# Six weight blocks of the merge's output product: high and low part made by two DMAs and a negation

## The chip, the core and the metric

One Trainium2 chip, one of its cores. The metric is device time in microseconds (us) of one execution of the whole program; lower is better. Differences between two kernels are told by the median of several runs.

## The reference, cut to what matters

The reference is one layer of a decoder trunk for 512 prompt tokens and 8 sample tokens (520 columns in the kernel, in two halves of 260). After RMSNorm, a wide projection `w_in` feeds two branches: retention with four heads (branch A) and a gated MLP with spatial mixing (branch B). Then comes the merge and the channel part:

```
m = sigmoid(a_ret) * branch_ret + sigmoid(a_gm) * branch_gm
h = x + m @ w_o                                   # 1024 x 1024, the product that the change touches
hn = rms_norm(h)
h = h + (silu(hn @ w_gate) * (hn @ w_up)) @ w_ffn_down
y = rms_norm(h)
```

All inputs are float32, and the kernel keeps nearly float32 accuracy.

## The kernel before, in words

**How a product is computed.** TensorE works on float32r numbers (float32 rounded to fewer bits). Each float32 operand is split into a high part (rounded to float32r) and a low part (the rounded difference), and `product` (L102) sums three matmuls: high by high, high by low, low by high. One block of 128 output rows with a contraction over 1024 takes 48 matmuls of 128x128 by 260 columns.

**How weights arrive.** `weights` (L92) takes three tiles of 128x1024 float32: SP loads 512 KB into `wraw` (L98), ScalarE casts it into `whi` (L87), VectorE writes raw minus high into `wlo` (L90). Tiles come from pools by turns (`wtile`, L77): in the stages around the change there are five buffers of `wraw` (three in pool `wp`, two in pool `wq`), four of `whi` and four of `wlo`. So the high and low buffers of block i come free when TensorE has ended block i-4.

**The stages around the change.** First the product with `w_gm_o`, eight blocks (loop at L709): VectorE multiplies each result by a gate (L715), GpSimd adds branch A (L717; VectorE does the last one), and the sum is split into `m`. Four marking matmuls follow (L840). Then comes the output product with `w_o`, eight blocks (loop at L841 to L851): `xr` is loaded (L843), the weights come from `weights` (L844), 48 matmuls into `ps_wo`, of which two PSUM tiles exist; VectorE adds x and writes `hs` (L849), ScalarE squares it and GpSimd adds the squares up (`add_square`, L162, L165, L167).

**What follows.** The feed-forward input product takes seven combined products per block (`sum_weights` L736, `sum_acts` L765, `seven` L815, `ffn_in` L868). `sum_weights` puts its raw data into buffers of the same kind `wraw`: `s13` into the three of `wp` (two SP loads of 256 KB, L749, and a GpSimd DMA of 512 KB that adds to them, L750) and `ab` into the two of `wq` (SP, L752). VectorE then makes further sums from both (L758, L759), and every sum is split into `whi` and `wlo`. `sum_acts` prepares the activations from `hs` (ScalarE fills at L855, VectorE sums at L793 to L807, splits). These start while the `w_o` product still runs.

**The order on each engine.** Each engine runs its instructions in one fixed order. It is laid down when the program is built: the framework plays the program through a timeline of its own (`schedule_with_timeline_sim=True`) and lets each engine take, of the instructions that are ready in that plan, the earliest in the program. On the chip, an instruction whose data is late holds up all that stand behind it on its engine; a DMA issued by GpSimd stands in GpSimd's order, one by SP in SP's.

Of the kernel before, what the change touches and what calls it, by code (L numbers as in the profile page):

```python
# [7 lines left out]
F32 = mybir.dt.float32  # L8
F32R = mybir.dt.float32r
I32 = mybir.dt.int32  # L10
AF = mybir.ActivationFunctionType
ALU = mybir.AluOpType
# [3 lines left out]
KT = D // P  # L16
# [19 lines left out]
def halves(ap):  # L36
    return ap.rearrange("p (a b) -> p a b", a=2)
# [3 lines left out]
def step_kernel(ctx: ExitStack, tc: tile.TileContext, io):  # L41
    nc = tc.nc
# [13 lines left out]
    def ttile(name):  # L56
        return tmp.tile([P, T], F32, name=name, tag="tmp")
# [10 lines left out]
    def acc_psum(name):  # L68
        return psm.tile([P, 2, 512], F32, name=name, tag="mm")
# [4 lines left out]
    def ev(ps):  # L74
        return ps[:, :, 0:HT]

    def wtile(kind, dt=F32R):  # L77

        pools = wpools[kind]
        pool = pools[wturn[kind] % len(pools)]  # L80
        wturn[kind] += 1
        return pool.tile([P, 8 * P], dt, name=kind, tag=kind, bufs=pools.count(pool))

    def split(hi, lo, src, hi_eng=None, lo_eng=None):

        if hi_eng is None:
            nc.scalar.copy(out=hi, in_=src)  # L87
        else:
            hi_eng.tensor_copy(out=hi, in_=src)
        (lo_eng or nc.vector).tensor_tensor(out=lo, in0=src, in1=hi.bitcast(F32), op=ALU.subtract)  # L90

    def weights(src, n, cuts=()):  # L92

        raw, hi, lo = wtile("wraw", F32), wtile("whi"), wtile("wlo")
        at = [0, *cuts, n]
        for a, b in zip(at, at[1:]):
            sl = slice(a * P, b * P)
            nc.sync.dma_start(out=raw[:, sl], in_=src[:, sl])  # L98
            split(hi[:, sl], lo[:, sl], raw[:, sl])
        return hi, lo  # L100

    def product(ps, w, at, x, first, last, fs=(0, 1)):  # L102

        sl = slice(at * P, (at + 1) * P)
        wh, wl = w[0][:, sl], w[1][:, sl]
        for n, (a, k) in enumerate(((wh, 0), (wh, 1), (wl, 0))):
            for f in fs:
                nc.tensor.matmul(  # L108
                    (ps[f] if isinstance(ps, list) else ps[:, f])[:, 0:HT], a, x[:, k, f * HT : (f + 1) * HT],
                    start=first and n == 0, stop=last and n == 2,  # L110
                )
# [50 lines left out]
    def add_square(acc, src, first, add=None):  # L162

        q = acc if first else stile("sqr")
        nc.scalar.activation(out=q, in_=src, func=AF.Square)  # L165
        if not first:
            (add or nc.gpsimd).tensor_tensor(out=acc, in0=acc, in1=q, op=ALU.add)  # L167
# [53 lines left out]
    def z_tile(m, name, w=None):  # L221
        w = w or weights(io["w_in"][m], KT)
        ps = acc_psum(name)
        for kt in range(KT):
            product(ps, w, kt, xg[kt], kt == 0, kt == KT - 1)
        return ps
# [7 lines left out]
    rsqrt_table(ones_f)  # L234
    x_load(0)
    w_first = [weights(io["w_in"][0], KT, (2, 4))]
    x_split(0)
    x_load(1)
    x_load(2)
    x_split(1)  # L240
    x_split(2)
    w_first.append(weights(io["w_in"][1], KT, (4,)))
    for kt in range(3, KT):
        x_load(kt)
# [464 lines left out]
    for i in range(KT):  # L709
        w = weights(io["w_gm_o"][i], KT)  # L710
# [130 lines left out]
    for i in range(KT):  # L841
        xt = ttile("xr")
        nc.sync.dma_start(out=xt, in_=io["xT"][i * P : (i + 1) * P, :])  # L843
        w = weights(io["w_o"][i], KT)  # L844
        ps = acc_psum("ps_wo")
        for kt in range(KT):
            product(ps, w, kt, mm[kt], kt == 0, kt == KT - 1)
        hi = hs[:, i, :]
        nc.vector.tensor_tensor(out=halves(hi), in0=ev(ps), in1=halves(xt), op=ALU.add)  # L849
        if i < KT - 1:  # L850
            add_square(sq, hi, i == 0)  # L851
# [53 lines left out]
    def down_weights(i, k0, n):  # L905
        return weights(io["w_ffn_down"][i][:, k0 * P : (k0 + n) * P], n)
# [28 lines left out]
    i = KT - 1  # L935
    hi = hs[:, i, :]
    ps = [aux(f"ps_fd{f}") for f in range(2)]
    w = down_weights(i, k0, n)
# [116 lines left out]
```

## Time and profile before

| | |
|---|---|
| median of 3 runs | 1140.57 us (1140.07 to 1145.29) |
| the profiled execution, its own time | 1138.51 us |
| its span from first to last instruction | 1136.8 us |
| mean granted TensorE clock | 0.996 of full speed |
| TensorE busy | 1113.2 us, 98% of the span |
| VectorE, ScalarE, GpSimd busy | 67%, 45%, 20% of the span |
| DMA, mean over the span | 145 GB/s |

The profile's times are in microseconds from the start of the span; durations of single instructions are in nanoseconds where so marked. PE is TensorE's matmul, PEld its weight load, DVE VectorE, ACT ScalarE, POOL GpSimd, SPq and POOLq the queues on which SP and GpSimd issue DMAs. A bracket behind a row of the timeline says how long the engine sat idle before the instruction, and what ended that. `L90` is line 90 of the kernel. Tiles go by the program's names, `s` being the tile `s13` or `s24` of `sum_weights`.

### The profile page before, as it was taken

The numbers are of one execution on the slowest core, as the hardware profiler recorded it, in microseconds if no ns is written. First come the engines' busy times: TensorE is split into PE (matmuls) and PEld (weight loads), VectorE is DVE, ScalarE is ACT, GpSimd is POOL, SyncE is SP. The second block draws the span as 40 slices with busy tenths as digits, with TensorE's granted clock in tenths as the row PEclk, the third lists the DMA queues.
The fourth block names the chain that finished last, engine by engine and source line by source line (L and its number), as shares of the span: only waits on it lengthen the run. The fifth ranks groups of instructions, "written<-read, shape, count | busy, mean of one in ns | idle before, by whom it ended". The sixth has DMA issues, their size and how long they took to land.

```text
span 1136.8 us, 21703 instructions
## 1 busy us (share of the span) xinstructions
PE 1113.2 (98%) x8982; PEld 1092.4 (96%) x8982; DVE 763.0 (67%) x1225; ACT 512.6 (45%) x836; POOL 224.7 (20%) x197
## 2 busy tenths in 40 slices
PE   8999999999999999999999999999999999999995
PEld 7999999999999999999999999999999999999995
DVE  7778837884878478737544446598776468755655
ACT  6356346533643356423332442366564145532552
POOL 4303201320132011001311222132332013210110
PEclk9999999999999999999999999999999999999998
DMA  7267335733673367222222323565654557446212
GB/s 272 96 217 291 107 117 210 266 110 112 230 245 110 112 219 282 87 94 97 82 75 93 102 78 109 159 140 139 173 161 150 145 118 187 136 132 147 80 42 76
DMA packets 54450, 164.82 MB, mean 145 GB/s; under 512 B 6432, under 2 KB 8880, under 8 KB 54344
## 3 DMA queue, kind: packets, MB, share of 16 engines
q1 hardware_dynamic: 43504, 124.53, 32.8%
q0 software_dynamic: 10848, 38.91, 12.6%
q8 instruction: 70, 1.15, 0.4%
q14 instruction: 28, 0.23, 0.1%
HBM read 142.32 MB, written 21.10 MB: 144 GB/s over the span
## 4 chain that ended last, share of the span: by engine, by line
PE 82%; DVE 8%; DMA 4%; issue 2%; ACT 2%; POOL 1%; SPq 0%; DVEq 0%; ACTq 0%; POOLq 0%
PE ps_f L827 14%; PE ps_fd L108 10%; PE ps_ro L108 8%; PE ps_v L108 8%; PE ps_g L108 7%; PE ps_gv L108 4%; PE ps_gu L108 4%; PE ps_ar L108 4%; PE ps_gm L108 4%; PE ps_ag L108 4%; PE k L108 3%; PE q L108 3%; PE ps_o L469 2%; DVE wlo L90 2%; PE ps_s L485 1%
## 5 line engine op out<-in xcount | busy, mean ns | idle before, releaser
L87 ACT CAST whi<-wraw 128x1024 fp32r<-128x1024 f32 (+3 forms) x139 | 141.3, 1018 | 273.2 <-issue 63.6
L90 DVE TENSOR_TENSOR wlo<-wraw,whi 128x1024 fp32r<-128x1024 f32 (+3 forms) x139 | 181.4, 1306 | 32.3 <-ACT whi L87 31.0
L108 PE MATMUL ps_fd<-act,whi 128*128 128x260 f32 x704 | 113.5, 282 | 1.2 <-DVE fd L915 0.6
L827 PE MATMUL ps_f<-hxh,whi 128*128 128x260 f32 x352 | 100.4, 286 | 3.1 <-DVE fb L886 1.0
L827 PE MATMUL ps_f<-hxh,wlo 128*128 128x260 f32 x352 | 98.7, 282 | 0.6 <-DVE wlo L90 0.6
L827 PE MATMUL ps_f<-hxl,whi 128*128 128x260 f32 x352 | 99.2, 282 | 0.0
L108 PEld LDWEIGHTS ps_fd<-act,whi 128*128 128x128 f32 x704 | 96.5, 188 | 2.2 <-ACT fb L893 1.2
L108 PE MATMUL ps_ro<-gated,whi 128*128 128x260 f32 x512 | 82.5, 283 | 0.0
L108 PE MATMUL ps_g<-xg,whi 128*128 128x260 f32 x512 | 82.4, 283 | 0.0
L108 PE MATMUL ps_v<-xg,whi 128*128 128x260 f32 x512 | 82.0, 282 | 0.0
L108 PE MATMUL ps_fd<-act,wlo 128*128 128x260 f32 x352 | 71.8, 282 | 0.0
L827 PEld LDWEIGHTS ps_f<-hxh,whi 128*128 128x128 f32 x352 | 66.2, 188 | 5.5 <-ACT fb L893 1.9
L108 PEld LDWEIGHTS ps_ro<-gated,whi 128*128 128x128 f32 x512 | 70.5, 188 | 0.8 <-issue 0.2
L108 PEld LDWEIGHTS ps_v<-xg,whi 128*128 128x128 f32 x512 | 69.9, 188 | 0.0
L108 PEld LDWEIGHTS ps_g<-xg,whi 128*128 128x128 f32 x512 | 69.8, 188 | 0.0
L451 ACT ACTIVATE kv<-qkb,vs 128x256 f32<-128x256 f32 x128 | 53.9, 498 | 30.1 <-DMA qkb<-qks 24.4
L827 PEld LDWEIGHTS ps_f<-hxh,wlo 128*128 128x128 f32 x352 | 65.9, 188 | 0.8 <-DVE wlo L90 0.8
L827 PE MATMUL ps_f<-hxm,whi 128*128 128x260 f32 x352 | 65.5, 283 | 1.0 <-ACT whi L87 1.0
L90 DVE TENSOR_TENSOR wlo<-s,whi 128x1024 fp32r<-128x1024 f32 x44 | 58.8, 1337 | 11.3 <-ACT whi L87 11.3
L827 PEld LDWEIGHTS ps_f<-hxl,whi 128*128 128x128 f32 x352 | 66.2, 188 | 0.0
L87 ACT CAST whi<-s 128x1024 fp32r<-128x1024 f32 x44 | 46.2, 1049 | 38.6 <-PE ps_f L827 17.6
L456 DVE SCALAR_TENSOR_TENSOR junk<-S,qkb 128x256 f32<-128x256 f32 x128 | 53.9, 421 | 2.2
(272 smaller groups left out, 2883.9 us busy)
## 6 DMA issues: line engine op xcount, KB each, us to landing
wraw<-in_w_in SPq DMA_DIRECT2D x78, 512.0 KB, 3.5
S<-in_st SPq DMA_DIRECT2D x32, 512.0 KB, 4.6
out_rss<-S POOLq DMA_DIRECT2D x32, 512.0 KB, 4.9
s<-in_w_ffn_in SPq DMA_DIRECT2D x44, 256.0 KB, 4.4
s<-in_w_ffn_in POOLq DMA_DIRECT2D x22, 512.0 KB, 6.3
ab<-in_w_ffn_in SPq DMA_DIRECT2D x22, 512.0 KB, 4.7
qkb<-qks POOLq DMA_DIRECT2D x16, 512.0 KB, 4.9
wraw<-in_w_ret_o SPq DMA_DIRECT2D x16, 512.0 KB, 3.5
```

Of the source, the lines that this page charges most:

```text
L87: nc.scalar.copy(out=hi, in_=src)
L90: (lo_eng or nc.vector).tensor_tensor(out=lo, in0=src, in1=hi.bitcast(F32), op=ALU.subtract)
L108: nc.tensor.matmul((ps[f] if isinstance(ps, list) else ps[:, f])[:, 0:HT], a, x[:, k, f * HT : (f + 1) * HT], start=first and n == 0, stop ...
L451: nc.scalar.activation(out=kv[:, j, :], in_=kb, func=AF.Copy, scale=vs[:, j, b : b + 1])
L456: nc.vector.scalar_tensor_tensor(out=junk, in0=S[:, j, :], scalar=1.0, in1=qb, op0=ALU.mult, op1=ALU.mult, accum_out=os_[:, j, b : b + 1],)
L469: nc.tensor.matmul(ps[:, s * P : NP], vtile(s, l)[:, j * P : (j + 1) * P], score(s, k), start=i == 0, stop=i == 11,)
L485: nc.tensor.matmul(ps, a[:, c // 2, ksl], vtile(c, l), start=i == 0, stop=i == 11)
L827: nc.tensor.matmul(bank[to], ww[:, sl], xx, start=to not in begun, stop=k == len(acts) - 1 and n == 2, skip_group_check=True,)
```

## The change

The blocks 2 to 7 of `w_o` no longer use `weights`. A new helper issues a GpSimd DMA that reads the float32 block from HBM and writes it rounded to float32r into `whi`; ScalarE writes minus `whi` into `wlo`; a second GpSimd DMA reads the same block once more and adds it to `wlo`. Blocks 0 and 1 stay as they were. The six blocks take no `wraw` buffer any more; `whi` and `wlo` go by turns as before.

```
+    def added_weights(src):
+
+        hi, lo = wtile("whi"), wtile("wlo")
+        nc.gpsimd.dma_start(out=hi, in_=src)
+        nc.scalar.activation(out=lo, in_=hi.bitcast(F32), func=AF.Copy, scale=-1.0)
+        nc.gpsimd.dma_start(out=lo, in_=src, accum_op=ALU.add)
+        return hi, lo
...
     for i in range(KT):
         xt = ttile("xr")
         nc.sync.dma_start(out=xt, in_=io["xT"][i * P : (i + 1) * P, :])
-        w = weights(io["w_o"][i], KT)
+        w = added_weights(io["w_o"][i]) if i >= 2 else weights(io["w_o"][i], KT)
```

## Rows read from the trace of the kernel before

**Rows 1.** The page, busy time, share of the span and instructions of each engine.
```profile
PE 1113.2 (98%) x8982; PEld 1092.4 (96%) x8982; DVE 763.0 (67%) x1225; ACT 512.6 (45%) x836; POOL 224.7 (20%) x197
```
**Rows 2.** Waits of PE, whole span: who for whom, us in total, times, longest.
```profile
PE ps_warm L233 <- DVE warm L230: 1.5, 1, 1.5
...
PE ps_f L827 <- ACT whi L87: 1.0, 1, 1.0
...
PE ps_f L827 <- DVE hs L849: 0.9, 1, 0.9
PE ps_wo L108 <- DVE hs L849: 0.8, 1, 0.8
PE ps_f L827 <- DVE wlo L90: 0.6, 1, 0.6
...
PE ps_f L827 <- ACT fb L893: 0.3, 1, 0.3
PE ps_v L108 <- DVE wlo L90: 0.3, 1, 0.3
```
**Rows 3.** Windows: length; busy PE, PEld, DVE, ACT, POOL; clock, DMA share, GB/s.
```profile
690.00:710.00 20.00, 20.00 (x170) 20.00 (x169) 12.01 (x11) 5.14 (x8) 3.93 (x3) 1.00 0.30 101
...
735.00:745.00 10.00, 9.25 (x78) 9.07 (x77) 9.24 (x14) 7.08 (x13) 2.71 (x2) 1.00 0.44 144
...
755.00:765.00 10.00, 9.66 (x82) 9.45 (x80) 9.96 (x15) 6.21 (x11) 2.83 (x3) 1.00 0.66 150
```
**Rows 4.** Timeline of ACT: start us, us, instruction.
```profile
709.91 1.05 ACT L87 CAST whi<-wraw 128x1024 fp32r<-128x1024 f32 x1 [2.72 <-PE ps_gm L108]
...
715.63 1.05 ACT L87 CAST whi<-wraw 128x1024 fp32r<-128x1024 f32 x1 [2.72 <-PE ps_gm L108]
...
743.20 0.64 ACT L165 ACTIVATE sqr<-hs 128x520 f32<-128x520 f32 x1 [0.82 <-DVE hs L849]
```
**Rows 5.** Tile ps_wo: durations in ns min/median/max, first and last start.
```profile
L108 PE MATMUL ps_wo<-m,whi x256: 277/281/387, 716.1 to 762.7; 128*128 128x260 f32 x128
```
**Rows 6.** Timeline of DVE, 710 to 766 us.
```profile
710.99 2.35 DVE L90 TENSOR_TENSOR wlo<-wraw,whi 128x1024 fp32r<-128x1024 f32 x1 [0.19 <-ACT whi L87]
...
723.20 1.23 DVE L90 TENSOR_TENSOR wlo<-wraw,whi 128x1024 fp32r<-128x1024 f32 x1 [0.19 <-ACT whi L87]
...
732.01 0.69 DVE L758 TENSOR_TENSOR s<-s,ab 128x512 f32<-128x512 f32 x1 [7.04 <-DMA ab<-in_w_ffn_in]
732.62 0.69 DVE L849 TENSOR_TENSOR hs<-ps_wo,xr 128x520 f32<-128x520 f32 x1
...
760.56 2.60 DVE L758 TENSOR_TENSOR s<-s,ab 128x512 f32<-128x512 f32 x1
...
764.70 0.68 DVE L849 TENSOR_TENSOR hs<-ps_wo,xr 128x520 f32<-128x520 f32 x1
```
**Rows 7.** DMA issues, 723 to 724 us: KB each, us to landing.
```profile
s<-in_w_ffn_in POOLq DMA_DIRECT2D x1, 512.0 KB, 8.0
```
**Rows 8.** Timeline of SP: DMA issues, merged.
```profile
690.46 23.24 SPq L98 DMA_DIRECT2D wraw<-in_w_o  x5
...
718.42 0.80 SPq L749 DMA_DIRECT2D s<-in_w_ffn_in  x2
...
724.45 0.33 SPq L752 DMA_DIRECT2D ab<-in_w_ffn_in  x1
```
**Rows 9.** Timeline of POOL.
```profile
710.94 1.31 POOL L717 TENSOR_TENSOR ms<-ms,br 128x520 f32<-128x520 f32 x1 [4.41 <-DVE ms L715]
...
745.99 0.87 POOL L750 DMA_DIRECT2D s<-in_w_ffn_in  x1 [3.72 <-DVE xsum L807]
746.59 1.62 POOL L167 TENSOR_TENSOR sq<-sq,sqr 128x520 f32<-128x520 f32 x1
```
**Rows 10.** The same view, whole span, median us to landing.
```profile
s<-in_w_ffn_in POOLq DMA_DIRECT2D x22, 512.0 KB, 6.3
...
qkb<-qks POOLq DMA_DIRECT2D x16, 512.0 KB, 4.9
...
wraw<-in_w_o SPq DMA_DIRECT2D x8, 512.0 KB, 3.4
...
out_rsp<-sf POOLq DMA_DIRECT2D x4, 512.0 KB, 3.2
```
**Rows 11.** DMA queues, 800 to 880 us: packets, MB, share of 16 engines.
```profile
q1 hardware_dynamic: 4098, 10.63, 40.7%
q0 software_dynamic: 576, 2.10, 16.4%
```

## The prediction

> **What bounds the kernel now.** I read the shares first: TensorE is busy 98% of the span [rows 1], so only what shortens or lengthens TensorE's waits counts. The view of PE's waits lists them all [rows 2]; from 1.5 us at the start down to 0.3; the fourteen lines come to 10.5 us of 1136.8. Three of them lie where the change works: 0.8 us in the w_o product and 0.9 and 0.6 us at the first feed-forward block. In each TensorE waits for VectorE. The windows say why [rows 3]: while w_gm_o is multiplied VectorE is busy 12.0 of 20 us and TensorE loses nothing; from 735 to 745 it is 9.24 of 10 and from 755 to 765 it is 9.96 of 10, and there TensorE drops to 9.25 and 9.66. ScalarE and GpSimd have room in both.
>
> The timelines of ScalarE and VectorE give the clockwork. A cast into whi starts when TensorE leaves a block: 709.91 and 715.63, so a block takes 5.72 us [rows 4]. The w_o product starts at 716.1 [rows 5]; its block 2 therefore at 716.1 + 2 x 5.72 = 727.6. VectorE stood 7.04 us, until 732.01, for the ab load of the feed-forward weights, and the eviction of w_o's block 1, ended at about 727.6, stood behind it until 732.62 [rows 6].
>
> **The change, part by part.** Durations are from the profiled execution, 1138.51 us (span 1136.8 and 1.7 around it), 2.1 us below the median 1140.57; the sum below is applied to both.
>
> *Removed from VectorE:* six subtractions of 1.23 us (2.35 for block 2's) [rows 6], 5 x 1.23 + 2.35 = 8.5 us. Two lie after 735, where VectorE is full.
>
> *ScalarE:* six casts of 1.05 us [rows 4] become six negations of the same shape. No row shows the negation; bounds are 0.64 us (a function on half the columns) and 1.05 for the cast with the same 1024 columns, which I take. Net nothing. But a negation waits for a DMA, and squares, fills and casts for hx stand behind it. The wait is at most the few us by which a DMA is later than planned; the activations that it holds are wanted by TensorE only from 763 on, and the last negation belongs near 747. I cost it at nothing; without that cover it would be up to 8.0 us once [rows 7].
>
> *SP:* six loads of 512 KB go [rows 8], and with them six turns of wraw. The last users of the five wraw buffers are then w_gm_o's blocks 5 to 7 and w_o's 0 and 1, whose subtractions end by about 708 (one block before the one at 710.99 [rows 6]). So the feed-forward loads that now issue at 718.42 and 724.45 [rows 8] can issue before 708, for three blocks of s13 and two of ab. That takes away the 7.04 us stand of VectorE [rows 6].
>
> *Added to GpSimd:* twelve DMA issues of 0.87 us [rows 9], 10.4 us on an engine busy 20%. Behind the first stands the addition at 710.94; 0.9 us later still puts that m pair well ahead of its use at the seventh eighth of block 0, 716.1 + 0.75 x 5.72 = 720.4. The additions of squares that queue behind are wanted only at the first feed-forward block. I cost the issues at nothing.
>
> *The new chain of a block:* whi comes free when block i-4 ends, at 709.9 for block 2, and is wanted at 727.6: 17.7 us. No row shows a rounding DMA. From below: 3.2 us, a plain 512 KB DMA of GpSimd; from above 8.0, the worst adding DMA [rows 7, 10]. I take 4.9, GpSimd's plain DMA that reads HBM, as the nearest [rows 10]. The adding DMA is measured: 6.3 in the median, 8.0 worst. With the handover of 0.2 and the negation of 1.05: 4.9 + 1.25 + 6.3 = 12.5 us, 5.2 to spare; at 8.0 for both 17.3, still inside. If each block's chain starts when its buffer is free, the cost is zero.
>
> **Sum.** The 0.8 us between 735 and 745 (a PSUM tile evicted late) [rows 2, 3] should go with the 7.04 us stand. Of the 0.9 + 0.6 at the first feed-forward block [rows 2], where the last eviction starts at 764.70 after a 2.60 us sum at 760.56 [rows 6], I take half, because the last block's own way through ScalarE and VectorE stays. 0.8 + 0.75 = 1.5 us; the bounds are 0 and 2.3. The profiled execution would become 1137.0, the median 1139.1 us.
>
> **Rivals.**
>
> *1. GpSimd's order turns serial (slower).* The order is fixed by a plan, and the plan takes transfers for shorter than they are: ab was expected before block 1's eviction and came 7.04 us late [rows 6]; on GpSimd an addition whose square was done at 743.84 stood until 746.59 behind an adding DMA that had to wait [rows 4, 9]. If the plan has block i's rounding landed and negated within 5.72 us, it puts the adding DMA ahead of block i+1's rounding DMA. On the chip GpSimd then stands at the adding DMA, and each block costs GpSimd the landing L, 1.25 and one issue of 0.87, so L + 2.1, against TensorE's 5.7. Block 2 starts with a spare of 17.7 - 1.25 - A - L (A the adding DMA); five further blocks each lose L - 3.6. With 4.9 and 6.3: 5.2 spare, 6.4 lost, 1.2 us late. With 6.3 for both, which is what the rounding costs if it goes like the addition: 3.8 spare, 13.5 lost, 9.6 late, 1139.1 + 9.6 = 1148.7. With 8.0 for both, about 21. It shows as slower by 0.5% from about 6 us for both. For it: the two rows named. Against: the early feed-forward loads leave the DMA engines quieter than the 8.0 row was, and the additions of squares fit into GpSimd's stand. The Trainium skill ("DMA: Bandwidth & Descriptors", section "Anatomy of one DMA") prices a GpSimd DMA at 2.0 us plus bytes over 436 GB/s, by estimate 3.2 us here; by that the cycle is 5.3 us and this rival costs nothing, but the adding DMAs of this trace took 6.3 and 8.0.
>
> *2. The DMA engines become the bound.* From the queue shares [rows 11], an adding DMA takes 16.4% of 80 us for four, 3.3 us of all engines; a plain 512 KB 40.7% of 80 us x 0.524 / 10.63, 1.6 us; the 260 KB of xr 0.8. A block then needs 3.3 + 1.6 + 0.8 = 5.7 us, just TensorE's pace, or 7.4 if rounding costs like adding: 6 x 1.7 = 10 us less the spare 5.2, about 5 us late, 1144. For it: every byte is read twice. The Trainium skill says against the change that DMAs issued by different engines run on the same 16 DMA engines and interleave (same page, "Issuing engines are not separate DMA queues"), so GpSimd's queue brings no bandwidth; that two kinds of transfers stretch each other fits the 8.0 us of the row at 723. Against: the window's mean DMA share is 0.44 to 0.66 [rows 3], and the feed-forward loads in it partly move ahead of 708.
>
> *3. Nothing moves.* The new plan leaves other late work in the same places: 1140.6.
>
> *4. More is gained.* If TensorE's waits of 0.8, 0.9, 0.6, 1.0 and 0.3 us in the w_o product and the first feed-forward block all went [rows 2], 3.6 us, it would be 1137.0; over 0.5% is out of reach of this stage, except by a reshuffle of the stages behind.
>
> **How the numbers follow.** Half a per cent (5.7 us) is about what a measurement can tell from no change. Chances: the forecast 0.50, rival 1 0.23 (of it 0.14 beyond 5.7 us), rival 2 0.10 (0.03 beyond), rival 3 0.13, rival 4 0.04 (0.03 beyond). Slower by over 0.5%: 0.17; faster: 0.03; within: 0.80. The range runs from the full gain and a little more, 1136.5, to rival 1 with a rounding DMA as dear as an adding one, 1148.5.
>
> **What would show it.** Right: no VectorE wait on ab near 725 to 732, feed-forward loads issued before 708, TensorE without its 0.8 us wait in the w_o product, no PE wait on a DMA in the w_o product. Wrong by rival 1: GpSimd's DMAs strictly in pairs, their distance over 5.7 us, PE waiting for wlo's DMA at the start of w_o's later blocks and longer each time. Wrong by rival 2: a DMA share near 1 from 715 to 760. A rounding DMA that lands after more than 8 us would break my bounds.

## The result and the profile after

The changed kernel took 1150.70 us in the median of 10 runs (1145.96 to 1156.52), the kernel before, beside it, 1142.32 us (1139.53 to 1146.19). The ratio is 1.006, with a 95% interval of 1.0043 to 1.0078: 0.006 x 1142.32 = 6.9 us slower, where 1.5 us faster was forecast. (The ratio is an estimate with its own interval and not the quotient of the two medians, which lie 8.4 us apart.) The profiled execution took 1145.96 us, the shortest of the ten, with a span of 1144.2.

Of the spans' difference, 7.4 us, not all lies where the change works: the first w_gm_o matmul starts at 669.8 us before and at 672.6 after, so 2.8 us are lost ahead of it (the last section says where). I therefore compare one stretch, from the marking matmuls (tile ps_mark) to the first down product (tile ps_fd); "the stage" means these two starts from here on. By tile, with the first and the last start behind the durations, the kernel before:

```profile
L840 PE MATMUL ps_mark<-m,ones_r x4: 281/283/285, 715.6 to 716.0; 128*128 128x260 f32 x4
L108 PE MATMUL ps_fd<-act,whi x704: 277/282/391, 866.8 to 1122.1; 128*128 128x260 f32 x176
```

The same two tiles of the changed kernel, whose lines behind the new function stand 8 further down (its L857 is L849 of before):

```profile
L848 PE MATMUL ps_mark<-m,ones_r x4: 281/283/285, 718.4 to 718.8; 128*128 128x260 f32 x4
L116 PE MATMUL ps_fd<-act,whi x704: 277/282/392, 874.4 to 1129.2; 128*128 128x260 f32 x176
```

The stage took 866.8 - 715.6 = 151.2 us before and 874.4 - 718.4 = 156.0 after: 4.8 us more.

The page of the changed kernel, busy times, answers to [rows 1]:

```profile
PE 1116.5 (98%) x8982; PEld 1095.2 (96%) x8982; DVE 749.6 (66%) x1219; ACT 512.2 (45%) x836; POOL 232.7 (20%) x209
```

VectorE has lost 13.4 us of work and six instructions, ScalarE's work is the same, GpSimd has its twelve issues and 8.0 us more. By busy time the work moved as planned, and the kernel is slower. The waits of PE say more. Changed kernel, 660 to 900 us: who for whom, us in total, times, longest.

```profile
PE ps_f L835 <- DVE hxl L90: 1.2, 1, 1.2
PE ps_f L835 <- DVE hs L857: 1.1, 1, 1.1
PE ps_f L835 <- ACT whi L87: 1.0, 1, 1.0
PE ps_wo L116 <- DVE hs L857: 0.8, 1, 0.8
PE ps_wo L116 <- DMA wlo<-in_w_o: 0.7, 1, 0.7
PE ps_f L835 <- DVE wlo L90: 0.6, 1, 0.6
PE ps_f L835 <- ACT fb L901: 0.3, 1, 0.3
PE ps_wo L116 <- DVE m L90: 0.2, 1, 0.2
```

They sum to 5.9 us; before, the same stretch had 0.8 + 0.9 + 0.6 + 1.0 + 0.3 = 3.6 [rows 2]. That is 2.3 of the 4.8. The rest shows in the windows (length; busy PE, PEld, DVE, ACT, POOL; clock, DMA share, GB/s) of the changed kernel. The second row is the stretch that [rows 3] have as 755 to 765, taken 2.8 us later; the last two lie behind the three waits at the first feed-forward block (the row at 625 us is for the last section):

```profile
625.00:630.00 5.00, 5.00 (x30) 4.98 (x30) 1.64 (x8) 0.00 (x0) 0.00 (x0) 0.66 0.29 97
...
757.80:767.80 10.00, 9.26 (x78) 9.05 (x77) 9.41 (x14) 7.36 (x15) 4.33 (x4) 1.00 0.59 157
...
770.00:775.00 5.00, 3.30 (x15) 2.91 (x16) 5.00 (x11) 4.46 (x11) 0.00 (x0) 0.78 0.54 143
775.00:780.00 5.00, 5.00 (x39) 5.00 (x38) 2.41 (x6) 1.98 (x4) 0.00 (x0) 0.88 0.06 22
```

VectorE's crowding ahead of the first feed-forward block has hardly eased, 9.41 us where [rows 3] had 9.96; ScalarE, 6.21 before, is now busy 7.36. And TensorE's granted clock, which stayed at 1.00 (2.4 GHz) after the waits of before, fell: half-microsecond windows show 0.50, the 1.2 GHz level, from 773.0 to 776.0, with TensorE busy all that time. By the two rows above that lost 5 x 0.22 + 5 x 0.12 = 1.7 us. Together 4.0 of the 4.8 us have a place.

Why the waits? GpSimd's timeline of the changed kernel (start, us, instruction, idle time before and what ended it; L105 is the rounding DMA, L107 the adding one):

```profile
726.24 0.86 POOL L107 DMA_DIRECT2D wlo<-in_w_o  x1 [1.76 <-ACT wlo L106]
726.78 0.88 POOL L105 DMA_DIRECT2D whi<-in_w_o  x1
731.14 0.55 POOL L105 DMA_DIRECT2D whi<-in_w_o  x1 [3.49 <-PE ps_wo L116]
736.24 0.86 POOL L107 DMA_DIRECT2D wlo<-in_w_o  x1 [4.55 <-ACT wlo L106]
...
739.62 0.86 POOL L107 DMA_DIRECT2D wlo<-in_w_o  x1 [1.19 <-ACT hxm L87]
740.19 0.87 POOL L105 DMA_DIRECT2D whi<-in_w_o  x1
...
748.20 0.84 POOL L107 DMA_DIRECT2D wlo<-in_w_o  x1 [3.90 <-ACT wlo L106]
748.79 0.84 POOL L105 DMA_DIRECT2D whi<-in_w_o  x1
```

Block 5's rounding DMA goes out at 731.14, when TensorE frees its buffer. The next buffers come free 5.72 us apart, near 736.9 and 742.6; the rounding DMAs of blocks 6 and 7 go out at 740.19 and 748.79, 3.3 and 6.2 us late, each directly behind an adding DMA that waited for a negation. GpSimd's order is what holds them. Two adding DMAs lie 748.20 - 739.62 = 8.6 us apart, where TensorE takes 5.72 for a block.

The negations wait for those DMAs, and ScalarE's other work stands behind the negations. ScalarE of the changed kernel, same columns:

```profile
734.88 1.06 ACT L106 ACTIVATE wlo<-whi 128x1024 fp32r<-128x1024 f32 x1 [7.31 <-DMA whi<-in_w_o]
735.84 0.62 ACT L173 ACTIVATE sqr<-hs 128x520 f32<-128x520 f32 x1
736.37 0.90 ACT L863 ACTIVATE xsum<-hs,gains 128x260 f32<-128x260 f32 x2
...
746.85 1.06 ACT L106 ACTIVATE wlo<-whi 128x1024 fp32r<-128x1024 f32 x1 [3.18 <-issue]
...
754.96 1.06 ACT L106 ACTIVATE wlo<-whi 128x1024 fp32r<-128x1024 f32 x1 [2.57 <-DMA whi<-in_w_o]
755.92 1.03 ACT L87 CAST whi<-ab 128x1024 fp32r<-128x1024 f32 x1
```

ScalarE stands 7.31 us until 734.88 with the square and the sum of an evicted row behind it. It stands again until 746.85; the profile names no releaser there, but block 6's rounding DMA, issued at 740.19, lands 6.6 us later, at 746.8. The last negation runs at 754.96, and the cast of the first feed-forward weights behind it at 755.92; before, that cast ran at 746.58, so it is 755.92 - 746.58 - 2.8 = 6.5 us later. VectorE, changed kernel, at the two ends of this:

```profile
703.06 0.69 DVE L766 TENSOR_TENSOR s<-s,ab 128x512 f32<-128x512 f32 x1 [0.77 <-DMA ab<-in_w_ffn_in]
...
737.30 1.43 DVE L808 SCALAR_TENSOR_TENSOR xsum<-xsum 128x260 f32<-128x260 f32 x1 [5.48 <-ACT xsum L863]
...
741.50 0.68 DVE L857 TENSOR_TENSOR hs<-ps_wo,xr 128x520 f32<-128x520 f32 x1
...
749.27 1.98 DVE L808 SCALAR_TENSOR_TENSOR xsum<-xsum 128x260 f32<-128x260 f32 x1 [4.07 <-ACT xsum L863]
...
754.03 0.69 DVE L857 TENSOR_TENSOR hs<-ps_wo,xr 128x520 f32<-128x520 f32 x1
...
770.74 0.69 DVE L857 TENSOR_TENSOR hs<-ps_wo,xr 128x520 f32<-128x520 f32 x1
```

The stand of 7.04 us for the ab load [rows 6] is down to 0.77, at 703. In its place VectorE stands 5.48 us until 737.30 for ScalarE's late sum, and the eviction of block 2, whose matmuls end near 736.9, follows only at 741.50. TensorE does not wait for that one, but the pattern comes again: VectorE stands 4.07 us until 749.27, the eviction of block 4 follows at 754.03, and block 6, which needs that PSUM tile, starts 0.8 us late for it. The last eviction starts at 770.74, 770.74 - 764.70 - 2.8 = 3.2 us later than in [rows 6], and TensorE waits for it and for the cast and difference of hx.

The DMAs themselves, changed kernel, issues from 690 to 770 us (KB each, median us to landing):

```profile
whi<-in_w_o POOLq DMA_DIRECT2D x6, 512.0 KB, 6.3
wlo<-in_w_o POOLq DMA_DIRECT2D x6, 512.0 KB, 5.5
```

### The profile page after: what moved, and what is told of

It reads as the page before. It is cut to its first block, busy times and chain, and to the rows that moved or that the text cites. A ratio compares the mean times of both kernels' runs of the same rounds, so it can differ in the third digit from the quotient of the medians.

```text
span 1144.2 us, 21699 instructions
## 1 busy us (share of the span) xinstructions
PE 1116.5 (98%) x8982; PEld 1095.2 (96%) x8982; DVE 749.6 (66%) x1219; ACT 512.2 (45%) x836; POOL 232.7 (20%) x209
## 4 chain that ended last, share of the span: by engine, by line
PE 76%; DVE 8%; issue 5%; DMA 5%; ACT 4%; POOL 1%; SPq 0%; DVEq 0%; ACTq 0%; POOLq 0%
PE ps_f L835 14%; PE ps_fd L116 11%; PE ps_ro L116 8%; PE ps_v L116 7%; PE ps_gu L116 4%; PE ps_g L116 4%; PE ps_ar L116 4%; PE ps_gm L116 4%; PE ps_ag L116 3%; PE ps_gv L116 3%; PE q L116 3%; PE k L116 3%; DVE wlo L90 2%; DMA S<-in_st 2%; DMA whi<-in_w_o 1%
## 5 line engine op out<-in xcount | busy, mean ns | idle before, releaser
L87 ACT CAST whi<-wraw 128x1024 fp32r<-128x1024 f32 (+3 forms) x133 | 135.0, 1017 | 251.8 <-issue 59.0
L90 DVE TENSOR_TENSOR wlo<-wraw,whi 128x1024 fp32r<-128x1024 f32 (+3 forms) x133 | 170.5, 1282 | 31.4 <-ACT whi L87 30.2
L461 POOL DMA_DIRECT2D out_rss<-S x32 | 17.0, 533 | 193.7 <-DVE S L460 193.7
```

The source lines that it names most:

```text
L461: nc.gpsimd.dma_start(out=io["rss"][b, h].rearrange("p (j d) -> p j d", j=NC), in_=S)
```

## The experiments

Each ratio is to the kernel before on the same chip, with its 95% interval; stage times are to be held against 151.2 us before and 156.0 after. One profile stands behind each stage time, and the changed kernel's own two gave 156.0 and 158.4 (e12), so a difference of a microsecond or two between stages says something only with the waits behind it. In some runs the clock fell to 0.50 within the stage; by half-microsecond windows TensorE's work lost 5.1 us by it in e2, 2.2 in e3, 6.2 in e4, 1.7 in e8 and 2.8 in e11, against 1.7 in the changed kernel and nothing in e1, e5, e7, e9 and e10. My theory was GpSimd's serial order together with ScalarE's stands; the main rival was that the DMA engines are full.

**e1_no_landing_wait.** The negation reads a tile that is there already, instead of whi, so the kernel leaves out the right low parts of the six blocks; the twelve DMAs stay.

```
         nc.gpsimd.dma_start(out=hi, in_=src)
-        nc.scalar.activation(out=lo, in_=hi.bitcast(F32), func=AF.Copy, scale=-1.0)
+        nc.scalar.activation(out=lo, in_=flat(mm[0].bitcast(F32)), func=AF.Copy, scale=-1e-3)
         nc.gpsimd.dma_start(out=lo, in_=src, accum_op=ALU.add)
```

> Edit: the negation on ScalarE reads a tile of m that is long there, scaled by -0.001, and not whi; same instruction count, same shapes, same DMAs, but nobody waits for the rounding DMA except TensorE (the low part of the six blocks is not computed as in the reference). Theory S (ScalarE and, behind it, GpSimd stand in their orders for the landing of the rounding DMA, the hx sums and the feed-forward weight casts behind come late): the stage from the marking matmuls to the first down product falls from 156.0 us back to 151 to 152.5, time 0.999 to 1.002 of before, and ScalarE shows no wait on whi's DMA. Rival D (the DMA engines are full, the parts themselves land late): traffic is the same, so 155 to 156 us and 1.005 to 1.007. Rival R (the early feed-forward loads and the new order do the harm): also 1.005 to 1.007.

Ratio 0.9983 [0.9963, 1.0004]; the stage is 870.2 - 721.4 = 148.8 us. Its window over the w_o product, and its DMA issues from 718 to 760 us:

```profile
715.00:765.00 50.00, 50.00 (x422) 50.00 (x421) 26.68 (x40) 27.01 (x45) 19.00 (x21) 1.00 0.81 208
```

```profile
whi<-in_w_o POOLq DMA_DIRECT2D x6, 512.0 KB, 7.8
wlo<-in_w_o POOLq DMA_DIRECT2D x6, 512.0 KB, 9.1
```

TensorE is busy 50.00 of 50 us (48.21 in the changed kernel), while the transfers landed later than in the changed kernel, 7.8 and 9.1 us against 6.3 and 5.5, and the DMA engines were busier, 0.81 against 0.75. So the loss is not one of bandwidth: it is gone as soon as no engine but TensorE stands until whi has landed.

**e2_negation_on_gpsimd.** The negation moves to GpSimd, so that ScalarE waits for no DMA.

```
-        nc.scalar.activation(out=lo, in_=hi.bitcast(F32), func=AF.Copy, scale=-1.0)
+        nc.gpsimd.tensor_scalar(out=lo, in0=hi.bitcast(F32), scalar1=-1.0, scalar2=None, op0=ALU.mult)
```

> Edit: the negation runs on GpSimd, so that ScalarE stands for no DMA; GpSimd stands as before and has six operations of some 1.5 to 2.5 us more. Theory S with ScalarE's stand as the harmful one: 0.999 to 1.003, stage 151 to 153.5 us. If GpSimd's stand (late low parts) is the harmful one: 1.006 to 1.012, stage 156 to 162, TensorE waiting for wlo's DMA. Rival D: 1.005 to 1.008.

Ratio 1.013 [1.0099, 1.016], stage 163.0 us. The negation takes 2.80 us on GpSimd and 1.06 on ScalarE, so a block's cycle on GpSimd grows, and TensorE's waits for wlo, 0.7 us in the changed kernel, become those that rival 1 named (this run, waits of PE from 660 to 900 us, then GpSimd's timeline):

```profile
PE ps_wo L116 <- DMA wlo<-in_w_o: 4.9, 3, 2.5
```

```profile
725.01 2.80 POOL L106 TENSOR_SCALAR wlo<-whi 128x1024 fp32r<-128x1024 f32 x1 [4.55 <-DMA whi<-in_w_o]
```

TensorE also waits 3.3 us for an eviction. The negation is dearer on GpSimd than the 1.5 to 2.5 us that I had allowed, so the run makes GpSimd's order costlier rather than taking ScalarE's share away cleanly.

**e3_rounded_early.** The rounded half lies in the wraw buffers, so that the rounding can start far ahead.

```
-        hi, lo = wtile("whi"), wtile("wlo")
+        hi, lo = wtile("wraw"), wtile("wlo")
```

> Edit: the rounding DMA of blocks 2 to 7 writes into a buffer of the kind wraw, which is free some 20 us before a whi buffer; the low part stays in wlo. Same DMAs, earlier start. The feed-forward loads then get their wraw buffers late again, as in the kernel before. Theory S: ScalarE's negations find the data there, 0.998 to 1.002, stage 150 to 152.5 us. Rival D: the bytes are the same in 25 us more of time, 1.002 to 1.006. Rival R (early feed-forward loads do the harm): 0.998 to 1.001 as well, so this run alone does not tell S from R.

Ratio 1.0099 [1.0073, 1.0124], stage 159.5 us, far from what I expected. The first five rounding DMAs did go out early, at 690.60 to 713.51, but TensorE holds the wraw buffers until a block is multiplied. So the feed-forward loads that should come early came late, and TensorE's longest wait, 7.4 us, is again for an eviction behind VectorE's stand for such a load (this run, VectorE):

```profile
775.43 0.69 DVE L766 TENSOR_TENSOR s<-s,ab 128x512 f32<-128x512 f32 x1 [5.69 <-DMA s<-in_w_ffn_in]
```

It trades the loss under study for one of the kind that the change had removed, and a larger one.

**e4_three_blocks.** Only blocks 5 to 7 are made by DMAs.

```
-        w = added_weights(io["w_o"][i]) if i >= 2 else weights(io["w_o"][i], KT)
+        w = added_weights(io["w_o"][i]) if i >= 5 else weights(io["w_o"][i], KT)
```

> Edit: only blocks 5 to 7 are made by the two DMAs; blocks 2 to 4 as in the kernel before. Theory G (GpSimd's serial order of rounding, landing, negation, adding is the cause, and its lateness grows from block to block): three blocks lose less than six, and the first has 5 us to spare, so 0.999 to 1.003 and a stage from the marking matmuls to the first down product of 150 to 153 us. Rival R (the harm comes with the early feed-forward loads, or with any GpSimd DMA put among the additions of squares): 1.003 to 1.006, about as after.

Ratio 1.0114 [1.0092, 1.0136], stage 165.1 us: worse than all six, and again not what I expected. The plan now puts a sum of feed-forward weights early on VectorE whose load is late (this run, VectorE), and TensorE waits 3.1 and 1.9 us for the m pair behind it:

```profile
728.31 0.69 DVE L766 TENSOR_TENSOR s<-s,ab 128x512 f32<-128x512 f32 x1 [10.34 <-DMA s<-in_w_ffn_in]
```

The three blocks' DMAs are in serial pairs again, but this other stand covers their price; the run says nothing on how the loss grows with the blocks.

**e7_gpsimd_order.** An ordering edge puts block i's negation and adding DMA behind the issue of block i+1's rounding DMA; the operations stay the same.

```
+        with tc.issue_after(nxt.ins) if nxt else nullcontext():
+            nc.scalar.activation(out=lo, in_=hi.bitcast(F32), func=AF.Copy, scale=-1.0)
+            nc.gpsimd.dma_start(out=lo, in_=src, accum_op=ALU.add)
...
+            ahead = rounded(io["w_o"][i + 1]) if i < KT - 1 else (None, None, None)
+            w = added_weights(src, hi, ahead[2])
```

> Edit: an edge puts the adding DMA of block i behind the rounding DMA of block i+1 on GpSimd, so that GpSimd never holds a rounding DMA back for a landing. Theory S: the rounding DMAs of blocks 4, 6 and 7 start 2 to 6 us earlier, ScalarE's stands shrink but do not vanish (it still comes to the negation about when the block is rounded): 1.000 to 1.004, stage 151.5 to 154.5. If GpSimd's serial order is the whole cause: 0.999 to 1.001. Rival D: 1.005 to 1.007.

Ratio 1.0004 [0.9982, 1.0027], stage 151.4 us. The interval lies below that of the changed kernel, so mending the order on GpSimd gives back about half a per cent, and TensorE no longer waits for hs, for hx or for wlo's DMA. The time fits both of my sentences, the theory's 1.000 to 1.004 and GpSimd's order as the whole cause, 0.999 to 1.001. What is left are ScalarE's stands for whi, 13.0 us in four (14.5 in four after): one of them holds the cast of the last m pair, for which TensorE waits 1.3 us. The stands are nearly as long as after but end sooner: the last negation starts 755.44 - 723.1 = 32.3 us behind the marking matmuls, 754.96 - 718.4 = 36.6 after.

**e8_order_and_vector_sum.** As e7, with one addition of w_gm_o's last blocks on VectorE, so that the last m pairs are ready before the negations.

```
-        add = nc.vector if i == KT - 1 else nc.gpsimd
+        add = nc.vector if i >= KT - 2 else nc.gpsimd
```

> Edit on the kernel with the edge on GpSimd: the addition of branch A for w_gm_o's block 6 moves from GpSimd, where it stood behind the feed-forward and rounding DMAs, to VectorE, as that of block 7 is already. Theory G: TensorE's 1.3 us wait for the cast of m goes, stage 149.5 to 150.5 us against 151.4, time 0.997 to 1.000 of before. If that wait only moves: 151 to 152, 1.000 to 1.002.

Ratio 1.0022 [1.0006, 1.0038], stage 153.0 us; TensorE's wait for the m cast grew to 1.9 us, and the 1.7 us of low clock behind it make up the 1.6 by which the stage is longer than e7's. The plan had put a negation ahead of the m cast, and the wait stayed with it (this run, ScalarE):

```profile
727.34 1.06 ACT L111 ACTIVATE wlo<-whi 128x1024 fp32r<-128x1024 f32 x1 [9.38 <-DMA whi<-in_w_o]
728.30 0.61 ACT L87 CAST m<-ms 128x520 fp32r<-128x520 f32 x1
```

**e9_gpsimd_stands_alone.** The other half: as e1, so that ScalarE waits for no DMA, but GpSimd copies one column of whi into lo ahead of the adding DMA, and so stands for the landing; the right low parts are left out again.

```
+        nc.gpsimd.tensor_copy(out=lo[:, 0:1], in_=hi[:, 0:1].bitcast(F32))
         nc.gpsimd.dma_start(out=lo, in_=src, accum_op=ALU.add)
```

> Edit on the run without the landing wait: ScalarE still fills the low part from a tile of m and waits for no DMA, but GpSimd copies one column of whi into the low part ahead of the adding DMA, so that GpSimd alone stands for the landing, in the order that the plan gives it (the low part is not the reference's). If GpSimd's stand is the cause: 1.003 to 1.008, stage 153 to 157 us. If ScalarE's stand is: 0.998 to 1.001, stage 149 to 151.

Ratio 1.004 [1.0017, 1.0062], stage 153.3 us: against e1, GpSimd's stand alone costs 4.5 us of the stage, with the clock at 1.00 throughout. GpSimd's timeline and the waits of PE, this run:

```profile
725.60 0.18 POOL L107 CAST wlo<-whi 128x1 fp32r<-128x1 f32 x1 [5.47 <-DMA whi<-in_w_o]
...
733.47 0.18 POOL L107 CAST wlo<-whi 128x1 fp32r<-128x1 f32 x1 [5.96 <-DMA whi<-in_w_o]
```

```profile
PE ps_wo L117 <- DMA wlo<-in_w_o: 1.9, 2, 1.5
PE ps_wo L117 <- POOL sq L176: 1.3, 1, 1.3
```

One block's cycle is 733.47 - 725.60 = 7.9 us, against TensorE's 5.72. The profile puts the 1.3 us down to an addition of squares, but the matmul that waits reads wlo, and block 4's adding DMA, issued at 742.20, lands 5.3 us later, just ahead of its start at 747.67; so I count it as a wait for wlo too, 3.2 us together. The plan's order here is not the changed kernel's: block 3's rounding DMA, which went out ahead of the first adding DMA there, stands behind it here. So e9 shows that GpSimd's stand is enough for a loss; its 4.5 us are not that stand's share in the changed kernel.

**e10_cast_before_negation.** e7 and a second edge: on ScalarE the negations come behind the last m cast.

```
         with tc.issue_after(nxt.ins) if nxt else nullcontext():
-            nc.scalar.activation(out=lo, in_=hi.bitcast(F32), func=AF.Copy, scale=-1.0)
+            with tc.issue_after(last_m.ins):
+                nc.scalar.activation(out=lo, in_=hi.bitcast(F32), func=AF.Copy, scale=-1.0)
```

> Edit on the kernel with the edge on GpSimd: a second edge puts the negations behind the cast of the last m pair on ScalarE, where that cast stood behind the first negation while it waited for whi's DMA. If ScalarE's stand cost TensorE the 1.3 us at block 0: that wait goes, stage from the marking matmuls to the first down product 149 to 150 us against 151.4, time 0.997 to 1.000 of before. If it only moves to another block: 151 to 152, 1.000 to 1.002.

Ratio 0.9983 [0.9961, 1.0004], stage 870.3 - 720.8 = 149.5 us. Waits of PE from 660 to 900 us, this run:

```profile
PE ps_f L842 <- ACT whi L87: 1.0, 1, 1.0
PE ps_f L842 <- DVE wlo L90: 0.5, 1, 0.5
PE ps_wo L123 <- DMA wlo<-in_w_o: 0.5, 1, 0.5
PE ps_f L842 <- ACT fb L915: 0.3, 1, 0.3
```

With the same operations and the same transfers, two edges take the whole loss away: what the change costs is the order in which two engines wait. ScalarE still stands 11.7 us for whi, but with nothing behind it that TensorE waits for. The step from e7 to e10 is within the intervals of the two ratios; it rests on the 1.3 us wait, which is gone.

**e5_early_loads_alone.** The gain by itself: the kernel before, casts and subtractions kept, with the raw halves of w_o's blocks 2 to 7 loaded into another tile, so that wraw is free for the feed-forward loads.

```
-        raw, hi, lo = wtile("wraw", F32), wtile("whi"), wtile("wlo")
+        raw = flat(wide("wown")) if own else wtile("wraw", F32)
+        hi, lo = wtile("whi"), wtile("wlo")
...
-        w = weights(io["w_o"][i], KT)
+        w = weights(io["w_o"][i], KT, own=i >= 2)
```

> Edit on the kernel before: the raw data of blocks 2 to 7 goes into the pool of the large tiles and takes no wraw buffer; casts and subtractions stay on ScalarE and VectorE. So the feed-forward loads come early as in the changed kernel, and nothing else changes. If the early loads are what gains in the run without the landing wait (151.2 to 148.8 us): 0.998 to 1.000, stage 149 to 150.5. If VectorE's relief is what gains: 1.000, stage 151. Rival R (early loads do harm): 1.003 to 1.006.

Ratio 0.9981 [0.9965, 0.9996], 1140.59 us against 1143.29 in the median: faster than both kernels, by 0.2% against the one before. The stage is 870.0 - 721.1 = 148.9 us, that of e1 to a tenth. PE's waits from 660 to 900 us are down to 1.0, 0.5 and 0.3 us, the same three as in e1. The feed-forward loads on SP, this run, which [rows 8] have at 718.42:

```profile
690.25 5.41 SPq L750 DMA_DIRECT2D s<-in_w_ffn_in  x4
```

All that e1 gains comes with the early loads, 2.3 us of the stage; the six subtractions taken from VectorE are worth nothing that these runs can tell, since e5 keeps them and its stage is as short.

**e11_early_loads_all_blocks.** As e5, with `own=True` for all eight blocks, to see whether still more is to be had.

> Edit on the kernel with the early loads alone: blocks 0 and 1 take their raw data from the large tiles too. If still earlier feed-forward loads have anything left to give: stage 147.5 to 148.5 us against 148.8, 0.997 to 0.999 of before. If the stage has no wait for data left: 148.8, 0.997 to 1.000. If the large tiles run short: 150 to 155, 1.001 to 1.005.

Ratio 1.0029 [1.0009, 1.005], stage 155.8 us. The chain of waits of this run has w_o's loads issued on SP only at 722.76, behind VectorE's next-to-last m pair; blocks 0 and 1 have no time for that, and TensorE waits 4.1 us for the first cast, with the low clock behind it (that row of the chain: start, us, what):

```profile
722.76 5.08 DMA wown<-in_w_o
```

**e12_changed_again.** The changed kernel once more, to see whether the fall of the clock recurs.

> The changed kernel once more, for a second profile. If the lower granted clock just behind TensorE's waits at the first feed-forward block belongs to those waits, it stands there again (about 0.8 to 0.9 in the five-us windows from 770, shifted with the start) and the stage is 155 to 157 us; if it is chance, it is absent and the stage 154 to 154.5.

One run, 1151.66 us; the stage took 158.4 us, 7.2 more than before, and PE's waits from 660 to 900 us came to 7.2 us, 3.6 more than before. Windows behind the first feed-forward block, this run:

```profile
775.00:780.00 5.00, 3.59 (x16) 3.18 (x15) 5.00 (x12) 4.47 (x12) 0.00 (x0) 0.50 0.52 143
780.00:785.00 5.00, 5.00 (x37) 5.00 (x36) 1.94 (x5) 1.71 (x3) 0.00 (x0) 0.81 0.03 12
```

The clock falls at the same place, from 2.4 to 1.2 GHz (0.50), for longer. TensorE was idle in part of that stretch, and those waits are counted already; its 3.59 and 5.00 us of work lost 3.59 x 0.50 + 5.00 x 0.19 = 2.7 us. So 3.6 + 2.7 = 6.3 of the 7.2 have a place.

## Why the prediction was wrong, point by point

The time lies above the range, on the side, slower by over 0.5%, that had 0.17. The step that failed is the sentence "If each block's chain starts when its buffer is free, the cost is zero": GpSimd's order kept the chains from starting then, and what TensorE lost came in good part by ScalarE's stands, which I had set at nothing. The mechanism is the first rival's, which had 0.23, joined to that second cost.

- **Early loads: right, and too small.** SP issues the feed-forward loads from 687.53 to 709.60; with the 2.8 us later start taken off, the last is at 706.8, ahead of the 708. The stand of 7.04 us is 0.77. In e5, where casts and subtractions stay, the waits of 0.8 and 0.9 us go and that of 0.6 is 0.5, 1.8 us where I took 1.5; the stage is 151.2 - 148.9 = 2.3 shorter, the upper of my bounds.
- **VectorE's 8.5 us of subtractions: too small as busy time, nothing as gain.** Its busy time fell by 13.4, with only these six instructions gone, so others ran shorter too; e5 with the subtractions and e1 without them have the same stage to a tenth.
- **"If each block's chain starts when its buffer is free, the cost is zero": the step that failed.** The condition does not hold. Blocks 6 and 7 started 3.3 and 6.2 us after their buffers came free, behind adding DMAs in GpSimd's order. In e7 the rounding DMAs of blocks 4 to 7 go out when their buffers come free, the latest 0.8 us after, and the ratio is 1.0004 in place of 1.006.
- **The rounding DMA: 6.3 us, not 4.9.** It costs what the adding DMA does, the upper of rival 1's two cases, beyond the "about 6 us" from which I had it decide. By the Trainium skill ("DMA: Bandwidth & Descriptors", section "Anatomy of one DMA") it would be 3.2 by estimate; the measurement decides, and it is about twice that. Block 2's chain ran from 715.77 to the landing of the adding DMA issued at 723.60, 5.4 us later: 13.2 us where I had 12.5, well inside the 17.7. So not the chain's length decided but its late start. (716.1 + 2 x 5.72 is 727.5 and not 727.6, which changes nothing. Block 2's own start was late too: 715.77, where its buffer came free at 709.9 + 2.8 = 712.7; GpSimd had stood 4.5 us for a feed-forward DMA. The 5.2 us to spare covered it.)
- **"I cost it at nothing" (the negation's wait on ScalarE): wrong.** I bounded it by 8.0 us once, and took the cover to be that hx is wanted only from 763 on and the last negation lies near 747. That negation ran at 754.96, 5.2 us past the 747 when the 2.8 are taken off, and ScalarE stood four times by name, 14.5 us in all, and a fifth time for 3.18, with sums behind it for which VectorE's L808 in turn stood 10.0 us in three. The two causes are linked: a late rounding DMA is also what ScalarE waits for, and with GpSimd's order mended the last negation comes 4.3 us sooner (e7). Over e1's 148.8 us lie the changed kernel by 7.2, e7 by 2.6 and e10 by 0.7: the edge on GpSimd gives back 4.6, of which 1.7 is the low clock, and that on ScalarE 1.9. How much each engine's stand would cost without the other's is not shown for the changed kernel's order.
- **Rival 1's price and its sign in the profile.** With 6.3 for both DMAs it gave 9.6 us; the stage of the changed kernel is 7.2 us over that of e1. The cycle is right: L + 2.1 with L = 6.3 is 8.4 us, and two adding DMAs lie 8.6 us apart. The total is near by luck, since the place is not right: I had TensorE waiting for wlo longer in each block, and it waited 0.7 us once. The pairs were not strictly serial, since the first two rounding DMAs went out ahead of the first adding one and block 5's ahead of block 4's, so behind adding DMAs the delay came to blocks 4, 6 and 7 alone (1.4, 3.3 and 6.2 us). Of TensorE's loss over e1, the larger part lies at the first feed-forward block, 2.4 us of waits behind VectorE and 1.7 of low clock, which no step of mine had.
- **Rival 2: refuted.** e1 has the same transfers, a share of 0.81 and landings of 7.8 and 9.1 us, and no loss. The rule that I set against the change, that GpSimd's queue brings no bandwidth of its own (the Trainium skill, "DMA: Bandwidth & Descriptors", section "Issuing engines are not separate DMA queues"), agrees with these longer landings; it was not what bound.
- **Not settled:** 0.8 of the changed kernel's 4.8 us (0.9 of the 7.2 in e12) have no wait or clock row of their own, and how the loss grows with the number of blocks stays open after e4.

## What to carry to other kernels

A DMA that must wait for a compute step, and a compute step that must wait for a DMA, are costed by what stands behind them on their engines, not by their own chain: here the same operations gave 1.006 or 0.9983, by two ordering edges. Where an order is planned from transfer times, hold those times against the trace, and put the next block's first DMA ahead of this block's second. And split a change into its parts: what gained here was a freed buffer that let later loads start early, which a few lines gave without the DMAs.

## What the runs showed that was not expected

- **Where the 2.8 us ahead of w_gm_o went.** The clock is at 0.50 from 8.5 to 15 us of the profile after and at 1.00 there before, but that cost nothing further on: the first ps_v matmul starts at 36.5 us after and 36.7 before. By the starts of TensorE's tiles, some 1.5 us are lost between 226 and 252 us, where the profile after has three waits for VectorE, 0.18, 0.33 and 0.42 us, that the one before lacks. Another 1.5 are lost between 625 and 670, where the row at 625 shows a clock of 0.66 (1.00 before): 5 x 0.34 = 1.7. Why the waits differ there is not shown.
- **The clock falls in other places too.** The kernel before in its first profile had a clock of 0.996; its other runs, beside the experiments, had 0.985 to 0.995. The profiles of e1, e5 and e12 also show less than 1.00 at 625, ahead of all that their edits touch.
- **Short waits can cost more than themselves.** In the changed kernel waits of 1.2, 1.1 and 0.6 us within 4 us were followed by a clock of 0.50, and so were longer ones in e12, e2, e3, e4, e8 and e11; in e1, whose waits there were shorter, the clock stayed at 1.00.
- **Three rounding and adding DMAs in flight land later than one.** Alone, an adding DMA of the changed kernel landed after 5.4 us (issued at 736.24) and a rounding one after 6.3 (731.14). Three issued close together, at 723.60, 726.24 and 726.78, landed after 5.4, 7.3 and 8.0 us; the later pairs, an adding and a rounding DMA half a microsecond apart, after 5.7 and 6.6 and after 5.4 and 6.1, hardly longer than alone.
- **Moving one part woke another stand in four runs** (e3, e4, e8, e11); in the first three it is the idle time in brackets in VectorE's or ScalarE's timeline, 5.69, 10.34 and 9.38 us, that names it.
